# Hybrid attention and mLSTM layer: FFN chunks of three and six token blocks, with Strassen's scheme in gate and up of the six

## The chip, the cores and the metric

One Trainium2 chip, one of its cores. The metric is the device time of one launch in microseconds; the median of three runs of the kernel before is 1618.27 us. Engines: TensorE (PE; PEld is its weight load), VectorE (DVE), ScalarE (ACT), GpSimd (POOL), and SyncE (SP), which issues most DMAs.

## The reference

One transformer layer is applied to 128 context tokens and to 1024 latent tokens, 1152 in all, of width 1024, in float32. Each group of tokens has its own modulation vectors (shift, scale, gate from SiLU of a condition). Cut to what matters:

```python
h = rmsnorm(x, norm1_w) * (1 + sc1) + sh1
aq, ak, av, mq, mk, mv, mo, mg = split(h @ w_in)         # attention and mLSTM inputs
attn_o = attention(rope(norm(aq)), keys, vals)           # 8 query heads of 64, 2 key heads
hm = rmsnorm(mlstm_both_directions(mq, mk, mv, mg)) * sigmoid(mo)
x = x + g1 * (concat([attn_o, hm]) @ w_out)
h2 = rmsnorm(x, norm2_w) * (1 + sc2) + sh2
g, u = split(h2 @ w_gu)                                  # each 1024 -> 2816
x = x + g2 * ((silu(g) * u) @ w_down)                    # 2816 -> 1024
y = rmsnorm(x, final_norm_w)
```

Latent tokens read 128 cached context keys and all 1024 latent keys; context tokens read context keys alone. The keys, values and mLSTM states of the context are outputs too.

## The kernel before

The 1152 tokens are nine blocks of 128 (block 0 is the context). A product of float32 matrices is done in three matmuls of pairs: each factor is split into a high part (`whi`, `aTh`; rounded to fp32r) and a low part (the rest), and high x high, high x low and low x high are added in PSUM. Helper `sub` (L135) computes the low part on VectorE or GpSimd, `load_piece` loads a weight piece into `raw`, copies the high part on ScalarE (L152) and calls `sub`.

Stages, in order: modulation (w_ada) and the first norm; the projection w_in head by head (`head_project`), beside which run the gates of the mLSTM, the rest of w_ada (`ada_rest`) and the mLSTM of the head before (`head_mlstm`); the queries; the mLSTM half of the output projection (`prefill`) beside the attention of the first three blocks. Then the FFN, in three chunks of three token blocks (`CB = 3`, 384 columns). A chunk goes over 22 blocks of 128 hidden features in the groups of `GROUPS`: `gate_up` makes gate and up of one feature block (two weight pieces, 8 k x 3 matmuls of 384 columns each), takes SiLU times up and splits the result into `hl`; `down` multiplies the group's features with w_down, 128 x 512 at a time, and adds the gated result to the residual `x1` (`add_gated`: L997 multiplies from PSUM, L998 adds).

The order of work is written out with generators. `weave(main, side, n_main, n_side)` runs the side's steps spread over the main's. Beside the first four groups of a chunk (17 feature blocks) runs the attention of the next chunk's three blocks; then `attn_out` (attention's half of the output projection), and the next chunk's second norm (`norm2`) beside the last group's `down`. `attention` computes for each head the scores `S` (L918, one buffer of three PSUM banks), the maximum (L920), exp (L921), the rounding to a float16 pair (L924, L925) and two DMA transposes (L928); the values (L942, L943) of a pair of heads come one pair later. The last chunk ends in `down_last`, which takes the last group's down products block by block and finishes each block's norm and store at once. `hot(n)` raises the priority of instructions; a scheduler in the build places each engine's instructions by a simulated timeline, and the order is then fixed.

Buffers are tags in pools: `b0` to `b5` in `hp` hold, one after the other, the first norm's output, the key stacks, the FFN's input pair (`b2`, `b3`) and the residuals (`b4`, `b5`). `raw` has two buffers, `whi` and `wlo` five each. PSUM is four banks `mm`, one `po` and three `S`.

```python
    for c in range(NCH):
        if c + 1 < NCH:
            main = groups(c, cur, GROUPS[:NG])
            ...
            weave(main, chain(previous(c, cur), att), 18 * sum(nf for _, nf in GROUPS[:NG]) - 24, 50)
            emit(att)
            emit(attn_out(c + 1, nxt, oT, out_gates()))
```

Of the kernel before, what the change touches and what calls it, by code (L numbers as in the profile page):

```python
# [8 lines left out]
F32 = mybir.dt.float32  # L9
# [28 lines left out]
LAST = [(0, 5), (5, 5), (10, 4), (14, 4), (18, 4)]  # L38
# [7 lines left out]
def hybrid_step(ctx: ExitStack, tc: tile.TileContext, I: dict, O: dict):  # L46
# [61 lines left out]
    x1_d = [drp.tile([P, D], F32, name=f"x1_d{i}") for i in range(CB)]  # L108

# [9 lines left out]
    def rsqrt(tp, ss, n, inv, cap=24, plus=EPS):  # L119
# [12 lines left out]
        return y  # L132
# [34 lines left out]
    vsc = cp.tile([P, 4], F32, name="vsc")  # L167

# [376 lines left out]
    def norm_rope(qp, cc, ss, x, nb, nh, w, rb):  # L545
# [6 lines left out]
        ssum = qp.tile([P, 20], F32, name=nm("nrs"), tag="nrs", bufs=2)[:, :n]  # L552
# [22 lines left out]
    def k_work(qp, cc, ss, kw):  # L575
# [7 lines left out]
        qone = qp.tile([1, P], F32, name="qone")  # L583
        dve.memset(qone, 1.0)
# [38 lines left out]
    mlp = es1.enter_context(tc.tile_pool(name="mlp", bufs=1, reuse_waits="tile"))  # L623
    mwh = mlp.tile([P, 512], F32, name="mwh")
# [165 lines left out]

    es_r = ExitStack()
# [6 lines left out]
    weave(head_project(1, sts[1]), beside((scan, 1.15), (ada, 0.45)), 56, 56)  # L798
    emit(scan)
    scan = head_mlstm(1, sts[1])  # L800
    weave(head_project(2, sts[2]), beside((scan, 1.15), (ada, 0.55)), 56, 56)
    emit(scan)
    emit(ada)
    es_r.close()
# [23 lines left out]
    kwork = k_work(qp, cc, ss, kw)  # L828
# [3 lines left out]
    emit(kwork)  # L832
    scan = head_mlstm(3, sts[3])
# [32 lines left out]
    ap = ctx.enter_context(tc.tile_pool(name="ap", bufs=1, reuse_waits="tile"))  # L866
    ap2 = ctx.enter_context(tc.tile_pool(name="ap2", bufs=1, reuse_waits="tile"))
    for name, bufs in (("mm", 4), ("po", 1), ("S", 1)):
        psum[name] = ctx.enter_context(tc.tile_pool(name="p" + name, bufs=bufs, space=PSUM, reuse_waits="tile"))
# [7 lines left out]
    def attention(c, oT, done, ha=200, hv=200):  # L877

        late = []
        for i in range(CB):  # L880
            b = c * CB + i
# [17 lines left out]
            for h in range(NQ):  # L899
# [33 lines left out]
                if h % 2 == 1:  # L933
                    def values(phT=phT, plT=plT, kv=kv, nk=nk, b=b, i=i, j=h // 2):
# [26 lines left out]
    att = attention(0, oT, done, 200, 100)  # L961
# [12 lines left out]
    def new_x1(c):  # L974
        x1 = hp.tile([P, CB, D], F32, name=nm("x1"), tag=f"b{4 + c % 2}")
        for i in range(CB):
            if c == 2:
                dma(x1[:, i, :], x1_d[i])
        return [x1[:, i, :] for i in range(CB)]
# [116 lines left out]
    def attn_out(c, a, oT, gs, gx=None, ready=None, then=None, ahead=None):  # L1096

        ws = None
        x1 = a["x1"]
        a["rs"] = []  # L1100
        for i in range(CB):
            while ready is not None and i not in ready:
                yield False
            b = c * CB + i
            if gx is None and i != 1:
                t = ap.tile([P, NQ, P], F32R, name=nm("mx"), tag="qT", bufs=1)
                th, tl = t[:, 0:4], t[:, 4:8]
            else:
                th, tl = mix_spare
            with hot(500):  # L1110
                o = oT[i]
                nc.scalar.copy(th, o)
                sub(tl, o, th.bitcast(F32), "dve" if gx is None else "pool")
            if then is not None and i > 0:
                yield from then(i - 1)
            yield True
            ws = ws or out_pieces(0, spare if gx is not None else None)
            for n in range(2):
                ps = out_block(ws, n, th, tl)
                with hot(200):  # L1120
                    add_gated(x1[i], ps, gx[n] if b == 0 else gs[n], n, pool if gx is not None else dve)
                yield True
            if then is not None:
                with hot(200):
                    a["rs"] += stats(x1[i : i + 1])
        if then is not None:
            yield from ahead
            yield from then(CB - 1)
        else:
            with hot(200):  # L1130
                a["rs"] = stats(x1)
# [9 lines left out]
    def norm2(c, a, i):  # L1141
# [8 lines left out]
        for half in range(2):  # L1150
            with hot(800):
# [6 lines left out]
                for j in range(4):  # L1158
                    k = half * 4 + j
                    if j == 0 and c == 0:  # L1160
# [8 lines left out]
                sub(tl[:, half * 4 : half * 4 + 4, i * P : (i + 1) * P], full, oh.bitcast(F32), "pool" if c == 0 else "dve")  # L1169
            yield True  # L1170

# [52 lines left out]

    def down(c, a, f0, nf, n):
# [26 lines left out]
    def down_last(c, a, f0, nf):  # L1252

        gs, ws = [], []
        fw = ap2.tile([P, D], F32, name="fw", tag="pr", bufs=2)
        dma(fw, I["final_norm_w"].rearrange("(o n) -> o n", o=1).to_broadcast([P, D]))
        for n in range(2):
            pieces = []
            for j in range(0, nf, 2):
                rows = w_down[(f0 + j) * P : (f0 + j + 2) * P, n * 512 : (n + 1) * 512].rearrange("(a p) n -> p a n", p=P)  # L1260
                pieces.append(load_piece([(full_view, rows)], (2, 512)))
            ws.append(pieces)
# [3 lines left out]
        for i in range(CB):  # L1266
            sl = slice(i * P, (i + 1) * P)
            st = ap.tile([P, 4], F32, name=nm("st"), tag="st", bufs=4)
            for n in range(2):
                ps = bank()  # L1270
                for k in range(nf):
                    wh, wl = ws[n][k // 2]
                    ah, al = a["act"][k][0][:, sl], a["act"][k][1][:, sl]
# [14 lines left out]
            nc.scalar.dma_start(yrow(c * CB + i)[:, 0:512], lo)  # L1288
            dma(yrow(c * CB + i)[:, 512:1024], hi)
# [7 lines left out]
    for n in range(2):  # L1297
# [6 lines left out]
                 attn_out(0, cur, oT0, gs, gx, done, lambda i: norm2(0, cur, i),  # L1304
# [8 lines left out]
    oT = []  # L1313
    att = attention(1, oT, set())
# [17 lines left out]
    def previous(c, a):  # L1332

        if c > 0:
            emit(finish(c - 1, a["prev"]))
            yield
        if c == 1:
            a["next"]["x1"] = new_x1(2)
            yield

    cur["next"] = nxt
    for c in range(NCH):
        if c + 1 < NCH:
            main = groups(c, cur, GROUPS[:NG])
            for _ in range(4):
                next(main)
            weave(main, chain(previous(c, cur), att), 18 * sum(nf for _, nf in GROUPS[:NG]) - 24, 50)
            emit(att)
            emit(attn_out(c + 1, nxt, oT, out_gates()))
            emit(groups(c, cur, GROUPS[NG:-1]))  # L1350
            f0, nf = GROUPS[-1]
            emit(gate_up(cur, f0, nf))
            n2 = chain(*[norm2(c + 1, nxt, i) for i in range(CB)])
            weave(chain(down(c, cur, f0, nf, 0), down(c, cur, f0, nf, 1)), n2, 6 * nf, 8)
            emit(n2)
            if c + 2 < NCH:
                oT = []
                att = attention(c + 2, oT, set())
            nxt["prev"] = cur
            cur = nxt  # L1360
            nxt = cur["next"] = {}
        else:
            main = groups(c, cur, LAST[:-1])
            for _ in range(4):
                next(main)
            weave(main, previous(c, cur), 24, 3)
            emit(main)
            emit(gate_up(cur, *LAST[-1]))
            down_last(c, cur, *LAST[-1])
# [52 lines left out]
```

## Time and profile before

| | |
|---|---|
| median of three runs | 1618.27 us (1617.77 to 1619.63) |
| the profiled execution | 1619.03 us, span 1617.1 us |
| mean granted TensorE clock | 0.977 |
| TensorE busy | 1532.5 us, 8670 matmuls |
| VectorE, ScalarE, GpSimd busy | 965.3, 689.8, 618.0 us |
| moved by DMA | 232.71 MB |
| FFN chunks, first product to last | 622 to 975, 977 to 1326, 1326 to 1604 us |

The span goes from the first to the last instruction. Busy time of TensorE counts a matmul from its start to a modelled end, and these overlap, so the pace of matmuls is read from the distance of their starts. A row of a timeline gives start and duration in us, engine, line and operation, output and inputs, shape, and in brackets how long the engine had been idle and for whom it waited.

### The profile page before, as it was taken

Reading aid. Unit: us, or ns where it says so; the run is one execution under the profiler, and the core shown is the slowest. Engines: PE = TensorE matmul, PEld = TensorE weight load, DVE = VectorE, ACT = ScalarE, POOL = GpSimd, SP = SyncE. Lnnn points to the kernel's source line nnn. Section 1 sums busy time; section 2 is a strip of 40 time slices with the busy share of each in tenths; the row PEclk is TensorE's granted clock in tenths of the full one; section 3 lists DMA queues with packets and bytes.
Section 4 is the critical chain, followed back from the end, with each engine's and each line's share of the span. In section 5 each row is a group of like instructions: output and inputs, shape, how many; then the busy total and the mean of one; then the engine's idle time right before and its main releaser. Section 6 shows DMA issues by size and latency. Waiting matters only on the chain. (4 is left out here: it accounts for less than half of the span.)

```text
span 1617.1 us, 23358 instructions
## 1 busy us (share of the span) xinstructions
PE 1532.5 (95%) x8670; PEld 1366.1 (84%) x8670; DVE 965.3 (60%) x1969; ACT 689.8 (43%) x1193; POOL 618.0 (38%) x392
## 2 busy tenths in 40 slices
PE   6899999899898968999999999999999999999996
PEld 2888888898676757998989899898898989999995
DVE  4842363957877668577663646767674474432445
ACT  3522242424534556555643344565552453333322
POOL 1511030413345324443445344444344445544443
PEclk8999999999898988999999999999999999999998
DMA  9244443303155865777773446777684445534441
GB/s 358 67 155 125 117 142 52 82 22 71 50 183 134 180 153 116 174 181 178 180 179 113 148 153 216 188 179 175 156 185 131 131 144 176 151 127 146 144 130 65
DMA packets 386311, 232.71 MB, mean 144 GB/s; under 512 B 169910, under 2 KB 346502, under 8 KB 386198
## 3 DMA queue, kind: packets, MB, share of 16 engines
q1 hardware_dynamic: 384342, 228.04, 52.5%
q10 hardware_dynamic: 1856, 3.19, 0.6%
q8 instruction: 68, 1.11, 0.3%
q14 instruction: 45, 0.37, 0.1%
HBM read 181.16 MB, written 11.69 MB: 119 GB/s over the span
## 5 line engine op out<-in xcount | busy, mean ns | idle before, releaser
L135 POOL TENSOR_TENSOR wlo<-raw,whi 128x1024 fp32r<-128x1024 f32 (+1 forms) x159 | 390.2, 2459 | 512.3 <-ACT whi L152 474.4
L152 ACT CAST whi<-raw 128x1024 fp32r<-128x1024 f32 x239 | 245.0, 1026 | 361.7 <-DMA raw<-in_w_gu_dram 112.8
L1190 PE MATMUL mm<-aTl,whi 128*128 128x384 f32 (+2 forms) x1088 | 363.6, 334 | 0.0
L1189 PE MATMUL mm<-aTh,whi 128*128 128x384 f32 (+2 forms) x1088 | 362.5, 335 | 0.8 <-DVE tn L1217 0.8
L1191 PE MATMUL mm<-aTh,wlo 128*128 128x384 f32 (+2 forms) x1088 | 363.2, 334 | 0.0
L1189 PEld LDWEIGHTS mm<-aTh,whi 128*128 128x128 f32 x1088 | 204.5, 188 | 2.2 <-DVE tn L1217 1.4
L1190 PEld LDWEIGHTS mm<-aTl,whi 128*128 128x128 f32 x1088 | 204.9, 188 | 0.7
L1191 PEld LDWEIGHTS mm<-aTh,wlo 128*128 128x128 f32 x1088 | 204.9, 188 | 0.2
L135 DVE TENSOR_TENSOR wlo<-raw,whi 128x1024 fp32r<-128x1024 f32 (+1 forms) x80 | 98.4, 1230 | 151.7 <-ACT whi L152 147.8
L1008 PE MATMUL mm<-whi,hl 128*128 128x512 f32 x372 | 146.4, 398 | 0.8 <-ACT hl L1221 0.7
L1009 PE MATMUL mm<-wlo,hl 128*128 128x512 f32 x372 | 146.9, 396 | 0.0
L1010 PE MATMUL mm<-whi,hl 128*128 128x512 f32 x372 | 144.3, 396 | 0.8 <-POOL hl L135 0.8
L399 PE MATMUL wi<-whi,hTh 128*128 128x384 f32 (+2 forms) x392 | 135.9, 347 | 5.2 <-ACT hTh L341 5.1
L925 DVE SCALAR_TENSOR_TENSOR pl<-pr,st,ph 128x1152 f16<-128x1152 f32 (+1 forms) x72 | 111.6, 1550 | 47.7 <-ACT ph L924 47.6
L401 PE MATMUL wi<-whi,hTl 128*128 128x384 f32 (+2 forms) x392 | 133.6, 343 | 1.3 <-POOL hTl L135 1.3
L400 PE MATMUL wi<-wlo,hTh 128*128 128x384 f32 (+2 forms) x392 | 133.5, 341 | 0.0
L921 ACT ACTIVATE pr<-S,st 128x1152 f32<-128x1152 f32 (+1 forms) x72 | 81.2, 1128 | 99.7 <-DVE st L920 90.6
L135 POOL TENSOR_TENSOR hl<-tn,hl 128x384 fp32r<-128x384 f32 x66 | 83.5, 1266 | 105.0 <-ACT hl L1221 104.9
L998 DVE TENSOR_TENSOR x<-x,t 128x512 f32<-128x512 f32 x102 | 116.9, 1168 | 0.8
L1217 DVE SCALAR_TENSOR_TENSOR tn<-tn,mm 128x384 f32<-128x384 f32 (+2 forms) x68 | 36.6, 539 | 134.2 <-PE mm L1191 100.4
L918 PE MATMUL S<-kst,qT 128*128 128x384 f32 (+1 forms) x400 | 88.1, 356 | 13.9 <-ACT pr L921 13.8
L920 DVE TENSOR_REDUCE st<-S 128x1 f32<-128x1152 f32 (+1 forms) x72 | 88.8, 1233 | 20.7 <-PE S L918 20.3
(323 smaller groups left out, 2714.2 us busy)
## 6 DMA issues: line engine op xcount, KB each, us to landing
raw<-in_w_gu_dram SPq DMA_DIRECT2D x132, 512.0 KB, 4.0
raw<-in_w_down_dram SPq DMA_DIRECT2D x60, 512.0 KB, 3.6
a<-in_w_ada_dram SPq DMA_DIRECT2D x32, 512.0 KB, 4.2
gl<-g_d SPq DMA_DIRECT2D x36, 256.0 KB, 3.8
aw<-in_w_ada_dram SPq DMA_DIRECT2D x16, 512.0 KB, 8.9
raw<-in_w_in_dram SPq DMA_DIRECT2D x32, 256.0 KB, 5.6
raw<-in_w_out_dram SPq DMA_DIRECT2D x15, 512.0 KB, 4.9
x<-in_x_sample_dram SPq DMA_DIRECT2D x13, 512.0 KB, 6.4
```

Of the source, the lines that this page charges most:

```text
L135: (dve if eng == "dve" else pool).tensor_tensor(out=out, in0=full, in1=hi, op=ALU.subtract)
L152: nc.scalar.copy(hi[:, :n], raw[:, :n])
L399: mm(ps[:, :n], ah, wh[:, k % 2, c0 : c0 + n], start=(k == 0), stop=False)
L400: mm(ps[:, :n], ah, wl[:, k % 2, c0 : c0 + n], start=False, stop=False)
L401: mm(ps[:, :n], al, wh[:, k % 2, c0 : c0 + n], start=False, stop=(k == KD - 1))
L998: eng.tensor_tensor(out=x1[:, cs], in0=x1[:, cs], in1=t, op=ALU.add)
L1008: mm(ps, ah, wh[:, k % 2, :], start=(k == 0), stop=False)
L1009: mm(ps, ah, wl[:, k % 2, :], start=False, stop=False)
L1010: mm(ps, al, wh[:, k % 2, :], start=False, stop=(k == nk - 1))
L1189: mm(ps, wh[:, k, :], th[:, k, :], start=(k == 0), stop=False)
L1190: mm(ps, wh[:, k, :], tl[:, k, :], start=False, stop=False)
L1191: mm(ps, wl[:, k, :], th[:, k, :], start=False, stop=(k == KD - 1))
```

## The change

The first chunk stays as it is (three blocks). The other six blocks become one chunk.

- Attention of all six blocks is woven into the first chunk; its output goes through DRAM (`o_d`). `attn_out_last` then does the output projection of six blocks, and `norm2_pair` the norms, block i with block i + 3.
- Gate and up of the six are a product of 2 x 2 blocks: the weights' columns are (gate, up), their rows the two halves of the 1024 inputs, and the tokens are two halves of 384. It is done by seven half products (4 k each, three float16 matmuls per k) in place of eight. `norm2_pair` makes the seven combinations of the activations once (`hc`), as float16 pairs; `combined` makes for every feature block the seven combinations of the weights; `gate_up_last` adds products in three PSUM banks and the rest by VectorE and ScalarE.
- The pairs are scaled by powers of two, from a bound of the activations and from the largest element of w_gu. `gate_up_max` reads all of w_gu (44 loads of 512 KB) beside the first heads' projections, `gate_up_scales` makes the factors (`gsc`).
- `down_six` uses each piece of w_down for six blocks; `down_last` has six blocks and the last two feature blocks. PSUM becomes eight banks `mm` after the attention.

```diff
-LAST = [(0, 5), (5, 5), (10, 4), (14, 4), (18, 4)]
+LAST = [(0, 4), (4, 4), (8, 4), (12, 4), (16, 4), (20, 2)]
+    def gate_up_max():
+        for t in range(44):
+            raw = wp.tile([P, 1024], F32, name=nm("raw"), tag="raw", bufs=2)
...
+                dma(raw, w_gu[k * P : (k + 1) * P, c * 1024 : (c + 1) * 1024])
...
+            dve.tensor_reduce(out=gmx[:, t : t + 1], in_=raw, axis=AX.X, op=ALU.max, apply_absolute_value=True)
+            yield
...
-    weave(head_project(0, sts[0]), beside((gates, 0.6), (ada, 0.45)), 56, 56)
+    weave(head_project(0, sts[0]), beside((gates, 0.6), (ada, 0.45), (gmax, 0.27)), 56, 56)
...
-    weave(head_project(3, sts[3]), beside((scan, 1.15), (kwork, 0.5)), 56, 56)
+    weave(head_project(3, sts[3]), beside((scan, 1.15), (chain(kwork, gscale), 0.5)), 56, 56)
...
+                            if b >= CB:
+                                dma(o_d[b - CB].rearrange("p (j x) -> p j x", j=4), oT[i])
...
+    def norm2_pair(tp, i, x1, rs, hc, sc, sh):
...
+            split("b11", b11, "pool")
+            sub(t1, b12, b11, "dve")
+            sub(t2_, b22, t1, "dve")
+            split("t2", t2_, "dve")
+            split("t1", t1, "pool")
...
+    def combined(f):
+        raws = []
+        for off in (0, D_FF):
+            raw = (wx if f % 2 else wp).tile([P, 1024], F32, name=nm("raw"), tag="raw", bufs=2)
...
+        w6 = hp.tile([P, 2, 6 * 512], F16, name=nm("w6"), tag=f"b{2 + f % 2}")
+        w1 = wx.tile([P, 2, 512], F16, name=nm("w1"), tag="w1", bufs=2)
...
+        for t in raws:
+            act(t, t, AF.Copy, scale=gsc[:, 1:2])
+        def split(w, cs, src, eng):
+            nc.scalar.copy(w[:, 0, cs], src)
+            sub(w[:, 1, cs], src, w[:, 0, cs], eng)
+        split(w6, slice(0, 1024), g, "pool")
+        dve.tensor_tensor(out=sa[:, lo], in0=u[:, lo], in1=u[:, hi], op=ALU.add)
+        sub(sa[:, hi], sa[:, lo], g[:, lo], "dve")
+        split(w6, slice(1024, 2048), sa, "dve")
+        sub(sb[:, lo], g[:, lo], u[:, lo], "pool")
+        sub(sb[:, hi], g[:, hi], sa[:, hi], "dve")
+        split(w6, slice(2048, 3072), sb, "dve")
+        split(w1, slice(0, 512), u[:, hi], "pool")
...
+    def seven(ps, w, h, first, last):
+        (wh, wl), t = w, h
+        for k in range(4):
+            mm(ps, wh[:, k, :], t[:, 0, k, :], ...)
+            mm(ps, wh[:, k, :], t[:, 1, k, :], ...)
+            mm(ps, wl[:, k, :], t[:, 0, k, :], ...)
+    def gate_up_last(a, hc, f0, nf):
...
+            if f + 1 < NF:
+                a["w"].append(combined(f + 1))
+            x, y, z = (bank()[:, 0:HT] for _ in range(3))
...
+            seven(x, w["a11"], hc["b11"], True, False)
+            nc.scalar.copy(c1, x)
+            seven(y, w["s2"], hc["t2"], True, False)
+            dve.tensor_tensor(out=u2, in0=y, in1=c1, op=ALU.add)
+            seven(z, w["s1"], hc["t1"], True, False)
+            nc.scalar.copy(p5, z)
+            seven(x, w["a12"], hc["b21"], False, True)
+            seven(y, w["s3"], hc["t3"], False, False)
+            dve.tensor_tensor(out=u3, in0=y, in1=c1, op=ALU.add)
+            seven(z, w["s4"], hc["b22"], False, True)
+            seven(y, w["a22"], hc["t4"], False, True)
+            dve.tensor_tensor(out=u2, in0=z, in1=u2, op=ALU.add)
+            dve.tensor_tensor(out=p5, in0=u3, in1=p5, op=ALU.add)
+            dve.tensor_tensor(out=c1, in0=y, in1=c1, op=ALU.add)
...
-            weave(main, chain(previous(c, cur), att), 18 * sum(nf for _, nf in GROUPS[:NG]) - 24, 50)
+    att = attention(range(CB, NB), [], set())
+    weave(main, att, 18 * sum(nf for _, nf in GROUPS[:NG]) - 24, 78)
+    emit(att)
...
+    n2 = chain(*[norm2_pair(np2, i, x1, rs, hc, sc[:, 0], sc[:, 1]) for i in range(CB)])
+    weave(gate_up(cur, f0, nf), n2, 6 * 2 * nf, 6)
+    weave(chain(down(0, cur, f0, nf, 0), down(0, cur, f0, nf, 1)), n2, 6 * nf, 6)
```

After the last sums `gate_up_last` takes, for each half of the tokens, tanh of the gate, one fused add and multiply, a scaled copy, a second fused multiply, the high part and the low part (on GpSimd).

More of the change, by code (lines that the diff above doesn't have):

```diff
@@ L108, in hybrid_step @@
     x1_d = [drp.tile([P, D], F32, name=f"x1_d{i}") for i in range(CB)]
+    o_d = [drp.tile([P, 512], F32, name=f"o_d{i}") for i in range(LB)]
     ident = cp.tile([P, P], F32, name="ident")
@@ L875, in hybrid_step, with attention @@
         sub(vs[:, i0 : i0 + 5, :, 1], v, vs[:, i0 : i0 + 5, :, 0], "pool")
-    def attention(c, oT, done, ha=200, hv=200):
+    def attention(blocks, oT, done, ha=200, hv=200):
         late = []
-        for i in range(CB):
-            b = c * CB + i
+        for i, b in enumerate(blocks):
             nk = 1 if b == 0 else NB
@@ L1094, in prefill, with attn_out @@
                     yield
-    def attn_out(c, a, oT, gs, gx=None, ready=None, then=None, ahead=None):
+    def attn_out(a, oT, gs, gx, ready, then, ahead):
         ws = None
@@ L1101, in attn_out @@
         for i in range(CB):
-            while ready is not None and i not in ready:
+            while i not in ready:
                 yield False
[L1104 to L1109, printed above, removed]
+            th, tl = mix_spare
             with hot(500):
@@ new lines, in hybrid_step @@
+    main = groups(0, cur, GROUPS[:NG])
+    for _ in range(4):
+        next(main)
+    weave(main, att, 18 * sum(nf for _, nf in GROUPS[:NG]) - 24, 78)
+    emit(att)
+    es_at.close()
+    psum["mm"] = ctx.enter_context(tc.tile_pool(name="p8", bufs=8, space=PSUM, reuse_waits="tile"))
+    np1 = ctx.enter_context(tc.tile_pool(name="np1", bufs=1, reuse_waits="tile"))
+    es_n = ExitStack()
+    np2 = es_n.enter_context(tc.tile_pool(name="np2", bufs=1, reuse_waits="tile"))
+    late_x1 = np1.tile([P, CB, D], F32, name="late_x1")
@@ new lines, in hybrid_step @@
+    for i in range(CB):
+        dma(late_x1[:, i, :], x1_d[i])
+    x1 = nxt["x1"] + [late_x1[:, i, :] for i in range(CB)]
+    pairs = [hp.tile([P, 2, 2, 4, HT], F16, name=nm("hc"), tag=f"b{i}") for i in range(2)]
+    hc = {"b11": pairs[0][:, 0], "t2": pairs[0][:, 1], "t1": pairs[1][:, 0], "b21": pairs[1][:, 1]}
+    for n in ("t3", "b22", "t4"):
+        hc[n] = np1.tile([P, 2, 4, HT], F16, name="hc_" + n)
+    sc = np1.tile([P, 2, KD], F32, name="sc")
+    dve.tensor_scalar(out=sc[:, 0], in0=scale2[:, :, 1], scalar1=gsc[:, 0:1], scalar2=None, op0=ALU.mult)
@@ new lines, in hybrid_step, with groups_last @@
+    emit(n2)
+    es_n.close()
+    wx = ctx.enter_context(tc.tile_pool(name="wx", bufs=1, reuse_waits="tile"))
+    last = {"x1": x1}
+    last["w"] = [combined(0)]
+    def groups_last():
+        for f0, nf in LAST[:-1]:
+            yield from gate_up_last(last, hc, f0, nf)
+            yield from down_six(last, f0, nf, 0)
+            yield from down_six(last, f0, nf, 1)
+    main = groups_last()
+    for _ in range(4):
+        next(main)
+    weave(main, finish(0, cur), 24, 3)
+    emit(main)
@@ L1372 @@
+    emit(gate_up_last(last, hc, *LAST[-1]))
+    down_last(last, *LAST[-1])
 TC_OPTS = dict(schedule_with_timeline_sim=True)
```

292 lines of the change are left out of this document (211 added, 81 removed).

## The prediction

> **What bounds the kernel now.** I read the page's busy times and slices first, then the table of stages, then the timeline of TensorE for the pace of single matmuls, then the engines beside it.
>
> ```profile
> span 1617.1 us, 23358 instructions
> ...
> PE 1532.5 (95%) x8670; PEld 1366.1 (84%) x8670; DVE 965.3 (60%) x1969; ACT 689.8 (43%) x1193; POOL 618.0 (38%) x392
> ...
> PE   6899999899898968999999999999999999999996
> ...
> PEclk8999999999898988999999999999999999999998
> ```
>
> The execution took 1619.0 us, 1.9 more than its span; the median of the runs is 1618.3, so a change of the span is taken over one to one. From slice 17 on (about 640 us) TensorE is busy all the time at full granted clock. The table of stages says the same (columns: busy us and instructions of each engine, clock, DMA share, GB/s):
>
> ```profile
> 80.00:120.00 40.00, 40.00 (x248) 32.65 (x247) 18.42 (x55) 9.75 (x24) 5.12 (x9) 1.00 0.53 165
> ...
> 280.00:320.00 40.00, 35.18 (x220) 31.87 (x218) 36.37 (x126) 17.80 (x61) 17.47 (x25) 1.00 0.26 71
> ...
> 560.00:600.00 40.00, 30.14 (x159) 24.59 (x158) 24.82 (x47) 23.00 (x30) 13.38 (x8) 0.83 0.76 177
> ...
> 1000.00:1040.00 40.00, 37.12 (x195) 32.32 (x194) 24.81 (x33) 20.68 (x26) 20.66 (x9) 1.00 0.78 223
> ...
> 1040.00:1200.00 160.00, 159.34 (x928) 147.00 (x927) 114.57 (x157) 92.80 (x121) 63.64 (x29) 1.00 0.74 174
> 1400.00:1560.00 160.00, 160.00 (x845) 149.71 (x844) 65.03 (x76) 52.53 (x66) 75.50 (x39) 1.00 0.44 135
> ```
>
> 1040 to 1200 is the second FFN chunk with the third chunk's attention woven in, 1400 to 1560 the third chunk alone. Both lose under 1 us of TensorE. Fewer or shorter matmuls there come off the end directly, as long as the other engines keep up. A busy TensorE can hide small gaps, so the pace is read from starts (start, us, engine, line):
>
> ```profile
> 1203.89 0.34 PE L1189 MATMUL mm<-aTh,whi 128*128 128x384 f32 x1
> ...
> 1213.60 0.34 PE L1191 MATMUL mm<-aTh,wlo 128*128 128x384 f32 x1
> ...
> 561.76 0.27 PE L942 MATMUL po<-phT,vs 128*128 128x256 f16 x1
> ...
> 563.40 0.27 PE L943 MATMUL po<-plT,vs 128*128 128x256 f16 x1
> ...
> 1601.34 0.39 PE L1274 MATMUL mm<-whi,hl 128*128 128x512 f32 x1
> ...
> 1603.90 0.40 PE L1276 MATMUL mm<-whi,hl 128*128 128x512 f32 x1
> ```
>
> 57 gate/up matmuls of 384 columns start in 9.71 us: 0.1734 us each. 16 float16 matmuls of 256 columns start in 1.64 us: 0.1093 each. 12 down matmuls of 512 columns: 0.2327 each.
>
> **The products.** Removed: two chunks x 22 feature blocks x 48 matmuls = 2112 at 0.1734, 366.2 us. Added: 22 x 7 half products x 4 k x 3 = 1848 float16 matmuls of 384 columns. No row has float16 at 384; the nearest, scaled by columns, gives 0.164 each, 303.1 us. Gain 63 us. If float16 were no faster than the present pairs at this size, 320.4 us and a gain of 46; if part of the 0.1093 is fixed per instruction, a little over 63. I take 63. The Trainium skill (TensorE: Matmul & The Clock Gate, Back-to-back issue gap) gives columns over 2.4 GHz plus 2.5 ns, 109.2 ns at 256, which the trace bears out; by it the 1848 would take 300 us and the gain be 66.
>
> Down products, output projection and attention keep their matmuls; only their order changes. With one FFN chunk fewer there is one change of chunk fewer: TensorE stood 2.9 us in 1000 to 1040. I count -3.
>
> **The vector work of the six-block chunk.** Strassen's sums replace matmuls by additions. Durations of their kinds, alone and beside GpSimd:
>
> ```profile
> 1400.13 1.05 ACT L152 CAST whi<-raw 128x1024 fp32r<-128x1024 f32 x1 [2.76 <-DMA raw<-in_w_gu_dram]
> ...
> 1404.50 0.51 ACT L1221 CAST hl<-tn 128x384 fp32r<-128x384 f32 x1
> ...
> 1404.67 2.40 POOL L135 TENSOR_TENSOR wlo<-raw,whi 128x1024 fp32r<-128x1024 f32 x1 [5.21 <-ACT whi L152]
> ...
> 1407.03 1.02 POOL L135 TENSOR_TENSOR hl<-tn,hl 128x384 fp32r<-128x384 f32 x1
> ...
> 1401.21 1.23 DVE L135 TENSOR_TENSOR wlo<-raw,whi 128x1024 fp32r<-128x1024 f32 x1 [4.32 <-ACT whi L152]
> ...
> 1402.36 0.55 DVE L1217 SCALAR_TENSOR_TENSOR tn<-tn,mm 128x384 f32<-128x384 f32 x1
> ...
> 1596.22 0.69 DVE L998 TENSOR_TENSOR x<-x,t 128x512 f32<-128x512 f32 x1
> ...
> 1597.78 1.81 DVE L998 TENSOR_TENSOR x<-x,t 128x512 f32<-128x512 f32 x1
> ...
> 1597.76 1.29 POOL L1283 TENSOR_TENSOR x<-x,fw 128x512 f32<-128x512 f32 x1 [7.30 <-ACT jk L1280]
> ```
>
> Per feature block TensorE needs 84 x 0.164 = 13.8 us of products. In `combined` and after the products GpSimd has one subtraction of 1024, two of 512 and two of 384: 2.40 + 2.58 + 2.04 = 7.0 us. VectorE has three sums of 512 (2.1), two splits of 1024 (2.5) and five two-input steps of 384 on SBUF (2.8), 7.3 us, and four sums that read PSUM (2.2). ScalarE: five passes of 1024 (5.3), about 0.6 for one of 512, eight of 384 (4.1): 10.0. Each engine alone fits in 13.8. But the pair of rows at 1597.8 shows an addition of two SBUF operands, 0.69 alone, take 1.81 when a GpSimd subtraction of 1.29 runs: it waited for it. If the two engines exclude each other so, 7.0 + 7.3 = 14.3 us stand against 13.8, and 16.5 if nothing of the PSUM sums fits beside GpSimd. Over a group of four blocks the down products (4 x 36 x 0.2327 = 33.5 us) add twelve additions (8.3) and four splits (some 8): 57.2 + 16.3 = 73.5 of 88.7 us of TensorE, so the mean fits, and one block's weights can be made ready during the down products, but the buffers b2/b3 hold two blocks' weights and no more. There is also a tight place: `u3` must leave bank y within the seven's 12 matmuls (2.0 us) before the next product adds to it, and VectorE, strictly in order, may stand behind a split or a wait for GpSimd; TensorE then waits, and all behind it. Bounds: 0 (in 1400 to 1560 VectorE and GpSimd together are busy 140.5 of 160 us and TensorE lost nothing) to 16.5 - 13.8 = 2.7 x 22 = 59 us. I take 0.8 us a block, 17 us, nearer to the first end because that row has the same kind of load.
>
> **Attention in one stretch.** Six blocks are now woven into chunk 0's first 17 feature blocks, 78 steps over the same main work where 50 were.
>
> ```profile
> L920 DVE TENSOR_REDUCE st<-S 128x1 f32<-128x1152 f32 (+1 forms) x72 | 88.8, 1233 | 20.7 <-PE S L918 20.3
> ...
> phT<-ph SPq DMA_TRANSPOSE x19, 3.4
> plT<-pl SPq DMA_TRANSPOSE x19, 4.5
> ...
> raw<-in_w_gu_dram SPq DMA_DIRECT2D x26, 512.0 KB
> raw<-in_w_down_dram SPq DMA_DIRECT2D x12, 512.0 KB, 3.6
> ```
>
> The transposes are those of 1040 to 1200, the loads those of 1400 to 1560. 19 heads in 160 us are 8.4 us a head. After: 17 x (48 x 0.1734 + 18 x 0.2327) = 212.7 us of FFN and 6 x (48 x 0.1734 + 72 x 0.1093) = 97 of attention, 310 us for 48 heads, 6.5 a head. A head costs VectorE (114.57 - 0.41 x 121.6) / 19 = 3.4 us, where 121.6 us is the FFN's share of those 160 (less 19 x 97 / 48) and 0.41 is VectorE's share in 1400 to 1560; the same way the DMA engines 3.4 (0.74 against 0.44). With the FFN beside it (4.4 us at 0.41 and 0.44) VectorE is at 5.2 of 6.5, DMA at 5.4. Both fit, but the slack between a pair's scores and its values shrinks by 4 us against a chain of reduce, exp, two roundings and a transposition of 4.5. Bounds: 0, as now, to 25 us (in 560 to 600, attention with little beside it, TensorE lost a quarter). I take 7.
>
> **The maximum of w_gu.** 44 loads of 512 KB and 44 reductions in 80 to 330 us. A load takes 0.44 x 160 / 39 = 1.8 us of the DMA engines (79 in all; the row of 80 to 120 has a share of 0.53, that of 280 to 320 one of 0.26); a reduction about 1.1 by the 1152 wide one (48 in all). VectorE has room in the first of these rows (18 of 40), hardly any in the second (36 of 40). SP issues these loads in order: one that waits for its `raw` buffer, that is for VectorE, holds the head weights and w_ada behind it. The scales' two reductions and dozen of short steps go into the same price. 0 to 20; I take 5.
>
> **The change of chunk.** `attn_out_last` has the matmuls of two `attn_out`; its loads of `o_d` and `late_x1` go beside 33 us of them. `norm2_pair` is woven into 62 us of chunk 0's last group. The first product needs all three pairs and the first combined weights, whose `w1` lies where norm2's tiles were. 0 to 8; I take 2.
>
> **The tail.** Six blocks with two feature blocks each, where there were three with four:
>
> ```profile
> 1587.41 0.39 PE L1274 MATMUL mm<-whi,hl 128*128 128x512 f32 x1
> ...
> 1599.52 0.68 DVE L997 TENSOR_TENSOR t<-mm,gl 128x512 f32<-128x512 f32 x1
> ...
> 1603.86 0.68 DVE L997 TENSOR_TENSOR t<-mm,gl 128x512 f32<-128x512 f32 x1
> ...
> 1612.63 0.75 DVE L1287 SCALAR_TENSOR_TENSOR x<-x,ry,fw 128x512 f32<-128x512 f32 x1
> ```
>
> Now the end comes 29.7 us after the first of these matmuls. TensorE's 16.8 us stay. VectorE takes 4.3 us a block (between the second and third row), more than the 2.8 us in which TensorE will deliver one: 2.8 + 5 x 4.3 + 9.5 (the last block's own chain, 1603.86 to 1613.38) + 3.7 to the end = 37.5, so +8; and with two feature blocks the last one's activations are wanted after a half, not three quarters, of the products. +6 to +16; I take +10.
>
> **Sum.** -63 - 3 + 17 + 7 + 5 + 2 + 10 = -25: 1594 for the profiled execution, 1593 for the median.
>
> **The rivals.** (a) All vector work hidden, no stall in the chunk and none in the attention: -63 - 3 + 2 + 2 + 8 = -54, 1564. For it: 140.5 of 160 busy and no loss today. Against it: only two weight buffers. (b) The pair VectorE and GpSimd sets the pace of the chunk of six: 16.5 us a block, +59 in place of 17, so +17: 1635, slower. It decides from 1.9 us a block on. For it: 1.81 for 0.69 beside GpSimd, and 14.3 against 13.8 even when packed. Against it: the down products' slack. The Trainium skill (SBUF — State Buffer, SBUF: two separate sides) calls this an exclusive lock held for a whole instruction, and those two rows agree. (c) Attention at 6.5 us a head no longer fits: TensorE loses 25 + 17 of the gain and the early stage its 20: 1626. (d) Float16 at 384 columns is no faster than now: 46 in place of 63, 1610.
>
> **How the numbers follow.** Forecast 0.45, (a) 0.23, (b) 0.20, (c) 0.06, (d) 0.06. About 0.2% (3 us) is what a measurement of this kernel can tell from no change. Forecast and (a), with most of (d), are faster: 0.71; 0.04 falls within 0.2%; slower 0.25. The range runs from (a) to just short of (b)'s full price: 1562 to 1632. The forecast's own range is 1575 to 1612.
>
> **What would show it.** Starts of the new products 0.162 to 0.165 apart, about 13.8 us a feature block. Waits of TensorE in the chunk of six, by VectorE's sums (y, u3) or by weights not yet split: 17 us in all; over 42 and (b) holds. Between chunk 0's start and its end, waits for `pr`, `phT` or `plT`: 7. From the first matmul of `down_last` to the end: 40 us. The forecast is wrong if the products start further apart than 0.17, if the six-block chunk's blocks take over 15.7 us, or if the stage before 450 us grows by more than 20.

## The result, and the profile after

The changed kernel takes 1719.19 us (median of four runs, 1712.37 to 1725.65) where the kernel before takes 1618.95 on the same chip: 1.0615 times as long, 95% interval 1.0564 to 1.0666. The forecast was 1593. It is slower by 100 us; even the top of the range, 1632, is far off.

The page of the changed kernel (its profiled execution took 1712.37 us):

```profile
span 1710.6 us, 23079 instructions
...
PE 1501.9 (88%) x8410; PEld 1196.6 (70%) x8410; DVE 1198.0 (70%) x2241; ACT 756.0 (44%) x1337; POOL 577.7 (34%) x394
...
PE   6898697889986887999999856996999999999993
...
PEclk8999899899998999999999967998999999999997
```

TensorE is busy 31 us less and VectorE 233 us more. The row of slices (42.8 us each, counted from 0) no longer has its unbroken stretch: there are new dips in slices 4 and 6 (171 to 299 us), in 23 and 24 (984 to 1069) and in 27 (1155 to 1197). The stages, in columns as before; the first row is the kernel before, all others the changed one:

```profile
160.00:200.00 40.00, 40.00 (x274) 35.18 (x269) 14.84 (x54) 7.51 (x26) 1.22 (x5) 1.00 0.40 109
```

```profile
160.00:200.00 40.00, 27.78 (x162) 23.70 (x160) 16.34 (x32) 1.14 (x3) 0.00 (x0) 0.90 0.84 182
```

```profile
735.00:960.00 225.00, 222.73 (x1280) 202.64 (x1279) 162.35 (x222) 130.18 (x170) 83.71 (x40) 1.00 0.84 184
960.00:1045.00 85.00, 46.87 (x229) 35.58 (x227) 47.99 (x74) 37.97 (x48) 7.94 (x4) 0.74 0.70 154
...
1153.00:1200.00 47.00, 34.07 (x175) 18.51 (x174) 44.76 (x58) 29.08 (x42) 20.96 (x13) 0.82 0.50 146
1200.00:1661.00 461.00, 443.77 (x2382) 296.11 (x2381) 345.42 (x403) 202.03 (x292) 194.19 (x110) 1.00 0.24 71
1661.00:1710.00 49.00, 20.37 (x90) 14.61 (x87) 36.03 (x115) 15.53 (x35) 9.61 (x8) 0.76 0.17 65
```

The reader is to see four places where TensorE stands: the early stage, 960 to 1045 (the end of the attention; the last product beside it is at 972), 1153 to 1200 (the change of chunk, with VectorE busy 44.76 of 47 us) and the tail. The long stretches, 735 to 960 and the six-block chunk from 1200, are nearly full.

I put a number on each place by the starts of TensorE's matmuls: length of the stage less the matmuls in it at their full pace (0.1627 us a float16 matmul of 384 columns, 0.1734 an fp32r one; a few records are missing, so these are rough).

| place | forecast | measured |
|---|---|---|
| 1848 float16 products for 2112 | -63 | -65 |
| one change of chunk fewer | -3 | -3 (taken as forecast, not measured apart) |
| maximum of w_gu: first gate/up product at 622.6 us before, 664.1 after | +5 | +41 |
| attention in one stretch (68 us lost in 664 to 1045, about 18 in the two such stretches before) | +7 | +50 |
| change of chunk (26 us lost in 1080 to 1200) | +2 | +24 |
| six-block chunk, 1200 to 1661 | +17 | +17 waits, +24 by the pace |
| tail, first down product of `down_last` to the end: 29.7 before, 49.1 after | +10 | +19 |

The right-hand column, with 24 for the chunk, adds to +90; the span of the two profiled executions grew by 93.5. The line at 1200 is drawn by hand: 18.6 of the 26 us of the change of chunk are lost from 1153.5 on, when the first feature blocks of the six-block chunk already run. Counted from there, the chunk lost 42 us.

The new products themselves do what was said of them:

```profile
1360.01 0.33 PE L1377 MATMUL mm<-hc,w 128*128 128x384 f16 x1
...
1365.37 0.33 PE L1377 MATMUL mm<-hc_t,w 128*128 128x384 f16 x1
```

The second start is the 33rd after the first: 5.36 us, 0.1624 each. (The Trainium skill, TensorE: Matmul & The Clock Gate, Back-to-back issue gap, gives 162.5 ns for 384 columns; the trace agrees.)

### The profile page after: what moved, and what is told of

Same layout as the page of the kernel before. It is cut to its first block, busy times and chain, and to the rows that moved or that the text cites. A ratio compares the mean times of both kernels' runs of the same rounds, so it can differ in the third digit from the quotient of the medians.

```text
span 1710.6 us, 23079 instructions
## 1 busy us (share of the span) xinstructions
PE 1501.9 (88%) x8410; PEld 1196.6 (70%) x8410; DVE 1198.0 (70%) x2241; ACT 756.0 (44%) x1337; POOL 577.7 (34%) x394
## 5 line engine op out<-in xcount | busy, mean ns | idle before, releaser
L138 POOL TENSOR_TENSOR wlo<-raw,whi 128x1024 fp32r<-128x1024 f32 x80 | 198.1, 2479 | 485.3 <-ACT whi L155 480.6
L155 ACT CAST whi<-raw 128x1024 fp32r<-128x1024 f32 (+1 forms) x121 | 124.3, 1031 | 119.8 <-DMA raw<-in_w_in_dram 38.6
L973 DVE SCALAR_TENSOR_TENSOR pl<-pr,st,ph 128x1152 f16<-128x1152 f32 (+1 forms) x72 | 112.4, 1561 | 52.2 <-ACT ph L972 51.8
L138 POOL TENSOR_TENSOR w<-raw,w 128x1024 f16<-128x1024 f32 (+1 forms) x44 | 91.7, 2086 | 159.1 <-ACT w L1357 155.9
L1303 PE MATMUL mm<-aTl,whi 128*128 128x384 f32 (+2 forms) x384 | 127.5, 332 | 0.0
L1304 PE MATMUL mm<-aTh,wlo 128*128 128x384 f32 (+2 forms) x384 | 127.2, 332 | 0.0
L1302 PE MATMUL mm<-aTh,whi 128*128 128x384 f32 (+2 forms) x384 | 126.9, 332 | 0.0
L1377 PE MATMUL mm<-hc,w 128*128 128x384 f16 x352 | 115.3, 330 | 5.7 <-ACT hc L1263 4.1
L1378 PE MATMUL mm<-hc,w 128*128 128x384 f16 x352 | 116.1, 330 | 0.0
L1379 PE MATMUL mm<-hc,w 128*128 128x384 f16 x352 | 115.3, 330 | 0.0
L1454 PE MATMUL mm<-whi,hl 128*128 128x512 f32 x240 | 93.2, 403 | 12.1 <-ACT hl L1426 7.4
L968 DVE TENSOR_REDUCE st<-S 128x1 f32<-128x1152 f32 (+1 forms) x72 | 88.8, 1233 | 18.7 <-PE S L966 18.0
L1044 DVE TENSOR_TENSOR t<-mm,gl 128x512 f32<-128x512 f32 x118 | 78.3, 683 | 30.7 <-PE mm L1089 11.2
L990 PE MATMUL po<-phT,vs 128*128 128x256 f16 x292 | 77.4, 296 | 22.5 <-DMA phT<-ph 11.6
```

Of the source, the lines that this page charges most:

```text
L138: (dve if eng == "dve" else pool).tensor_tensor(out=out, in0=full, in1=hi, op=ALU.subtract)
L155: nc.scalar.copy(hi[:, :n], raw[:, :n])
L1302: mm(ps, wh[:, k, :], th[:, k, :], start=(k == 0), stop=False)
L1303: mm(ps, wh[:, k, :], tl[:, k, :], start=False, stop=False)
L1304: mm(ps, wl[:, k, :], th[:, k, :], start=False, stop=(k == KD - 1))
L1377: mm(ps, wh[:, k, :], t[:, 0, k, :], start=(first and k == 0), stop=False, skip_group_check=True)
```

## The experiments

All are the changed kernel with the edit shown. Each time is a median of four runs, each ratio one to the kernel before, which ran beside it (1619 to 1621 us); 1.0615 is the changed kernel. Two ratios differ if their intervals do not meet.

### The maximum of w_gu

**No maximum.** The 44 loads and reductions replaced by `dve.memset(gmx[:, 0:44], 0.17)`; the scale then doesn't come from the data.

> The changed kernel without the 44 loads and reductions for the largest weight; the maximum is set to the constant 0.17, so the scale is not taken from the weights. Theory (the maximum costs the stage of the head projections 42 us, the distance by which the first gate/up product came later): about 1677 us, first gate/up product near 622 us, not 664. Rival (that stage was late for another reason, such as the smaller buffers of the square roots): it stays near 1719.

1689.24 us, 1.0427 (1.0412 to 1.0443): 30 us back, 12 fewer than the first expectation. The first gate/up product comes at 634.2, where 622 was expected.

**Reductions without loads, loads without reductions.**

```diff
-            dma(raw, w_gu[...]); dve.tensor_reduce(out=gmx[:, t : t + 1], in_=raw, ...)
+            dve.tensor_reduce(out=gmx[:, t : t + 1], in_=<1024 numbers of hTh[0]>, ...)   # first kernel
+            dma(raw, w_gu[...])                                                           # second kernel
```

> The 44 reductions stay on VectorE at their places, but they read a part of the first norm's output that lies in SBUF; nothing is loaded, so the scale is taken from other numbers. Theory (VectorE, in order, stood with a reduction at its head that waited for its load: 70 us of idle time before the reductions): most of the 42 us come back, about 1680 to 1690, and the reductions wait for nothing. Rival (the 54 us of VectorE work itself delays the mLSTM's steps): 1705 or more.

> The 44 loads stay, the reductions go, the maximum is the constant 0.17. Theory (VectorE's wait): 1677 to 1690. Rival (the 22 MB on the DMA engines, or SP standing at a load that waits for its buffer with the head weights behind it): 1705 or more. If both this and the run without loads come near 1680, neither the work nor the loads cost it alone, and it is the wait of the one for the other.

Reductions alone: 1708.98 us, 1.0536 (1.0517 to 1.0556). Loads alone: 1721.12, 1.0626 (1.0602 to 1.0649), as slow as with both. So the loads are enough to cost it all. The first of the two is less clear than it looks: with nothing to wait for, the reductions were placed in one lump, and TensorE lost time at another place than in the changed kernel (below). The first gate/up product comes at 642.0, 8 us later than in the run without a maximum. That run is 20 us faster in all; where the other 12 us go is open.

```profile
80.00:120.00 40.00, 29.79 (x181) 26.57 (x180) 40.00 (x46) 5.50 (x12) 4.98 (x9) 0.87 0.47 142
```

**Small loads.** As loads alone, but each brings 64 of its 1024 columns: `dma(raw[:, 0:64], w_gu[k * P : (k + 1) * P, c * 1024 : c * 1024 + 64])`.

> The 44 loads for the maximum stay in their places, in the same queue and the same two raw buffers, but each brings 32 KB instead of 512 KB, and the reductions are left out (the maximum is a constant, as in the run with loads alone, 1721). If the moved bytes cost the time (the DMA engines busy 0.84 to 0.92 at 160 to 200 us), the queries end near 470 us and the kernel takes 1685 to 1695, like the run without any of it (1689). If the order in SyncE's queue or the shared raw buffers cost it, nothing comes back: queries end near 495 to 510, 1712 to 1725.

1705.54 us, 1.0523 (1.0489 to 1.0557). Neither expectation holds: half of it comes back. What the main DMA queue moved from 80 to 330 us (packets, MB, share of 16 engines) in the kernel before, the changed kernel, and this one:

```profile
q1 hardware_dynamic: 40987, 27.85, 40.7%
```

```profile
q1 hardware_dynamic: 40445, 47.36, 70.3%
```

```profile
q1 hardware_dynamic: 43828, 27.50, 41.6%
```

The bytes are back to those of before, and the first gate/up product comes at 650.4, between 634.2 (none) and 660.4 (whole loads): some 10 to 16 us are the bytes (by this start, and by the times) and 16 are the places that the loads hold.

**Another queue.** `dma` for these loads became `nc.scalar.dma_start`, so that no head weight stands behind them on SyncE.

> As the changed kernel, but the 44 loads for the maximum are issued by ScalarE, so that no head weight stands behind them in SyncE's queue; bytes, raw buffers and reductions stay. If the order in SyncE's queue is the cost, the queries end 20 us or more earlier than 509 us and the kernel takes 1690 to 1700. If it is the bytes or the two raw buffers, 1710 to 1728, and ScalarE's own waits may add some.

1722.99 us, 1.0648 (1.0622 to 1.0673): nothing back. This does not clear the order in SyncE's queue, since the waits moved along with the loads. From 80 to 330 us, in the changed kernel, SyncE stands at these loads (L800), and everything issued after them with it:

```profile
SPq L800 <- DMA raw<-in_w_gu_dram: 50.5, 22, 7.5
...
SPq L800 <- DVE gmx L804: 15.7, 15, 1.6
```

With the loads on ScalarE's queue, ScalarE's own steps wait behind them, and the head weights (L154, still on SyncE) wait for a `raw` buffer that the loads hold:

```profile
ACT kt L654 <- DVE gmx L804: 25.1, 2, 16.2
...
ACT part L377 <- DMA raw<-in_w_gu_dram: 21.4, 1, 21.4
```

```profile
SPq L154 <- DMA raw<-in_w_gu_dram: 18.3, 3, 13.0
SPq L154 <- DVE gmx L804: 16.2, 3, 14.3
```

So both kinds of place are seen to hold something up, a queue's order and the two shared buffers; how the 16 us divide between them stays open. Loads with buffers of their own were not tried.

**The maximum from chunk 0's own pieces.** No extra loads: `load_piece` in chunk 0 takes one more `dve.tensor_reduce` of each raw piece of w_gu, and the weights' factor is made after the last.

> The 44 extra loads are gone: the maximum is taken from the raw weight pieces of w_gu that chunk 0 loads anyway (44 reductions on VectorE in 665 to 1120 us), and the weights' factor is made after the last of them. If the extra loads were the cost of the early stage, it comes back as in the run without any maximum (first gate/up product near 634 us) and the kernel takes 1692 to 1703. If VectorE's reductions beside the attention lengthen each head's chain (above 7.6 us a head), half of that is lost again: 1704 to 1716.

1736.9 us, 1.0716 (1.0687 to 1.0745): worse than both expected. The early stage came back in part (first gate/up product at 645.6, where 634 was expected), but chunk 0 paid more than that: this is an experiment on the attention, below.

### The attention

**More cover.** The last group's gate and up of chunk 0 is put beside the attention as well: `chain(groups(0, cur, GROUPS[:NG]), gate_up(cur, *GROUPS[-1]))`, and norm2 beside that group's `down` alone.

> The gate and up products of chunk 0's last group (five feature blocks, 41 us of TensorE) are put beside the attention too; the second norms of the six blocks then go beside that group's down products alone. Theory (attention cannot go faster than 7.5 us a head beside the FFN, so 62 us of it were left over with TensorE half idle from 960 to 1045): some 35 to 40 us of these are covered; the norms lose 5 to 15 of cover: 1690 to 1705. Rival (the rest of the attention is slow of itself, by the transposes): no gain, 1715 or more.

1706.56 us, 1.0529 (1.0513 to 1.0544): 13 back, between the two expectations. Two heads are left over when the gate/up products end (1028), where there were 13 (943); but norm2 then lacks its cover, and the first Strassen product comes only 8 us earlier (1145.5).

**Attention written denser.** 112 steps in place of 78 over the same products: `weave(main, att, ... - 24, 112)`.

> The six blocks' attention is woven into chunk 0 at 112 steps where 78 were, nothing else. If the heads left over at 972 us are there because the products were written ahead of them, heads come some 6 us apart, none is left over, and 25 to 35 us come back: 1685 to 1695. If a head's own chain of waits (scores, reduce, exp, rounding, transposition, one S buffer) sets 7.5 us a head beside the products, nothing moves: 1710 to 1722.

1735.89 us, 1.0726 (1.0708 to 1.0744): slower by 17, outside both expectations. One maximum (L968) is taken for each head; the groups' rows count them in 735 to 940 us, in the changed kernel and in this one:

```profile
L968 DVE TENSOR_REDUCE st<-S 128x1 f32<-128x1152 f32 x27 | 36.4, 1349 | 1.3 <-PE S L966 1.2
```

```profile
L968 DVE TENSOR_REDUCE st<-S 128x1 f32<-128x1152 f32 x25 | 33.8, 1351 | 8.8 <-PE S L966 8.7
```

27 heads in 205 us are 7.6 us a head. Written denser they are no closer, 8.2. By the starts of its matmuls, TensorE loses 27 us from the first gate/up product to the last product beside the attention, 17 in the changed kernel; its longest waits there are at the value products, 7.7 us in all. The heads cannot be hurried from there.

**No low part of the probabilities.** Leaves out per head the VectorE pass L973, one transposition and 9 matmuls.

> Leaves out the low parts of the probabilities: per head one VectorE pass (1.4 to 2.1 us), one DMA transposition (1.3 to 1.9) and 9 matmuls of 0.109 us. The chain scores, maximum, exp, next scores stays. If that chain sets the 7.5 us a head beside the products, heads stay at 7.0 or more and the time falls little: 1698 to 1716. If VectorE's or the DMA engines' load sets it, heads come at 6.3 us or less, none is left over, and the kernel takes 1645 to 1670.

1699.19 us, 1.0492 (1.0476 to 1.0508), at the edge of the chain's 1698 to 1716. The same row, 735 to 940 us:

```profile
L966 DVE TENSOR_REDUCE st<-S 128x1 f32<-128x1152 f32 x27 | 36.6, 1354 | 30.9 <-PE S L964 30.7
```

VectorE now waits 30.7 us for scores, and yet there are 27 heads again. Neither VectorE's nor the DMA engines' load sets the pace. The products end at 946 instead of 972, since 292 matmuls are gone, and 11 heads are left over then, 10 in the changed kernel; the time that came back needs no faster head. In the run with chunk 0's maximum the count is 24 (8.5 us a head):

```profile
L960 DVE TENSOR_REDUCE st<-S 128x1 f32<-128x1152 f32 x24 | 32.4, 1349 | 4.1 <-PE S L958 4.0
```

Its 21 other reductions there stand between links of the chain in VectorE's fixed order, 1.2 us each and 15.9 us of waiting for the weights that they read:

```profile
L157 DVE TENSOR_REDUCE bcol<-raw 128x1 f32<-128x1024 f32 x21 | 25.5, 1215 | 15.9 <-DMA raw<-in_w_gu_dram 15.9
```

One head of the changed kernel (timeline):

```profile
900.50 1.29 PE L966 MATMUL S<-kst,qT 128*128 128x384 f32 x6
...
902.82 1.35 DVE L968 TENSOR_REDUCE st<-S 128x1 f32<-128x1152 f32 x1
...
904.20 1.23 ACT L969 ACTIVATE pr<-S,st 128x1152 f32<-128x1152 f32 x1 [0.90 <-DVE st L968]
...
908.28 1.22 PE L966 MATMUL S<-kst,qT 128*128 128x384 f32 x6
```

Scores, maximum and exp take 1.3, 1.4 and 1.2 us; 1.0 goes by behind a pass on VectorE, and 2.8 until TensorE, in its written order, comes to the next scores. `S` has one buffer, so no head starts before the exp of the one before. Of the 7.6 us some 2 come with the products: the ten heads that are left over at 972 follow each other 5.5 us apart, though TensorE then runs at a lower clock (0.74).

### The change of chunk and the tail

**Group of two first, `finish` later.** `LAST = [(0, 2), (2, 4), (6, 4), (10, 4), (14, 4), (18, 4)]`, and `finish` starts 12 steps later.

> In the six-block chunk the group of two feature blocks comes first instead of last, and the end of chunk 0 (finish) is written 12 steps later. If the tail's extra is the last activations coming late and the 7 us wait at 1175 is finish's vector steps, the last down products to the end take 40 to 43 us where 49 were and the first Strassen products 10 us less: 1695 to 1706. If the tail is paced by VectorE's 4.3 to 4.9 us for each of six blocks and the wait is only passed on, 1710 to 1720.

1709.07 us, 1.0561 (1.0529 to 1.0593); the interval meets that of the changed kernel, so the gain of 10 is not sure, and the time lies between the two expectations. The tail takes 51.3 us, but now holds 33.5 us of down matmuls where it held 16.8. Waits of TensorE from 1125 to 1300 us, total, times and longest:

```profile
PE mm L1377 <- DVE u L1404: 4.8, 1, 4.8
PE mm L1377 <- ACT hc L1263: 4.0, 1, 4.0
PE mm L1379 <- DVE w L138: 3.3, 1, 3.3
PE mm L1454 <- ACT c L1418: 3.3, 1, 3.3
```

In the changed kernel the first of these was 7.3 and the second 4.1. With `finish` out of the way other steps of VectorE fill its place.

**No GpSimd in the chunk's gate and up.** Leaves out GpSimd's low parts of a11, a12, a22 and of the activations in `hl`, and its sum of 512; the high part is multiplied twice, so all matmuls stay. The expectation below names b11, t1, b21 and b22 too, but the edit does not touch `norm2_pair`: the trace still has its 12 steps on GpSimd, and the low parts of w_down are left there as well.

> Leaves GpSimd's subtractions out of the six-block chunk's gate and up and of its norm (the low parts of a11, a12, a22, b11, t1, b21, b22 and of the activations, and one sum of 512): the high part is used twice there, so the number of matmuls stays. VectorE keeps its own steps, less none. If VectorE and GpSimd holding each other up is what the stalls of the chunk (16.9 us of TensorE waits after 1200) and the 24 us at the change of chunk come from, 20 to 35 us come back: 1685 to 1699. If the waits are the order of the steps on VectorE and ScalarE's last step before the down products, at most 12: 1707 to 1722.

1683.65 us, 1.0408 (1.0377 to 1.044): 35 us back, as much as the first expectation had at most; between the profiled executions it is 30. The first Strassen product comes at the same time (1153.4), which says nothing of the norm, whose GpSimd steps stayed; the last comes 26 us earlier. The wait of 7.3 us for `u` is gone, and the waits from 1200 on fall from 16.9 to 6.7. VectorE's groups, 1153 to 1661 us, in the changed kernel:

```profile
L1417 DVE SCALAR_TENSOR_TENSOR tn<-tn,p 128x384 f32<-128x384 f32 x21 | 29.3, 1393 | 7.9 <-ACT tn L1416 7.9
...
L138 DVE TENSOR_TENSOR sa<-sa,raw 128x512 f32<-128x512 f32 x22 | 28.0, 1277 | 0.4
...
L1404 DVE TENSOR_TENSOR u<-mm,c 128x384 f32<-128x384 f32 x22 | 12.2, 553 | 39.0 <-PE mm L1379 39.0
...
L1484 DVE SCALAR_TENSOR_TENSOR x<-x,ry,fw 128x512 f32<-128x512 f32 x6 | 8.9, 1550 | 0.0
```

and with those steps left out (two of the rows are one line further down):

```profile
L138 DVE TENSOR_TENSOR sa<-sa,raw 128x512 f32<-128x512 f32 x22 | 17.2, 784 | 0.4
...
L1418 DVE SCALAR_TENSOR_TENSOR tn<-tn,p 128x384 f32<-128x384 f32 x22 | 15.8, 720 | 7.2 <-ACT tn L1417 7.1
...
L1405 DVE TENSOR_TENSOR u<-mm,c 128x384 f32<-128x384 f32 x22 | 12.2, 555 | 50.5 <-PE mm L1380 50.5
...
L1484 DVE SCALAR_TENSOR_TENSOR x<-x,ry,fw 128x512 f32<-128x512 f32 x6 | 4.1, 748 | 0.0
```

The same steps with two operands in SBUF take 1393, 1277 and 1550 ns beside GpSimd's steps and 720, 784 and 748 without them; the step that reads one operand from PSUM takes 553 and 555.

### All together

Chunk 0's maximum, more cover, the group of two first, `finish` later; then the same with a constant for the maximum.

> Chunk 0's maximum, chunk 0's last gate and up beside the attention too, the group of two first and finish later, all together. If the three losses are separate, their gains add: 1719 - 20 to 30 - 13 - 10 = 1666 to 1676. If they hide each other (a stage only waits for the next late thing), 1680 to 1695. In neither case below before's 1619.

> As the run before it, but with a constant in place of the maximum: no loads and no reductions for it at all. It shows what the maximum still costs there. Gains that add: 1719 - 30 - 13 - 10 = 1666, within 1660 to 1672; the 44 reductions in chunk 0 then cost 0 to 10.

1714.62 us, 1.0587 (1.0556 to 1.0617), missing both expectations, and 1665.17, 1.0281 (1.0264 to 1.0299), as the sum of the single gains said (1666). As far as this sum shows, the losses are separate and add. The 49 us between the two are the maximum's, for which 0 to 10 was expected: the last head's scores start at 1044 in the one and 1001 in the other, and the first Strassen product comes at 1164.2 and 1113.7. The reductions in chunk 0 are not all of it, since TensorE also stands for the factor that is made after the last of them:

```profile
PE mm L117 <- DVE gt L1593: 12.5, 1, 12.5
```

Not even the one without a maximum comes near the kernel before.

## Why the prediction was wrong, point by point

**The products: right.** 0.164 was taken, 0.1624 measured, and the gain is 65 us. Rival (d) is out.

**The maximum of w_gu: the largest miss in proportion.** The term was "0 to 20; I take 5"; the early stage grew by 41 us, past the 20 named as what would make the forecast wrong. I added up what the DMA engines and VectorE had free over 250 us and found room. The stage has its own order instead: the head weights go through the same queue and the same two `raw` buffers, and they come late, partly by the bytes (10 to 16 us), partly by the places that the loads hold there (16). Of the 41, 30 go with the maximum. The other 11 lie between the queries' end (468.0 us without the maximum, 465.8 before, by the start of its last product) and the first gate/up product (634.2 and 622.6); their cause is open.

**Attention: the step that failed is "Both fit".** The term compared loads, VectorE 5.2 and DMA 5.4 of 6.5 us a head. Heads came 7.6 us apart beside products whatever was taken off either engine; that this is the pace of a chain is by exclusion of the two loads. 24 heads in 205 us were to be counted in the trace of before:

```profile
L920 DVE TENSOR_REDUCE st<-S 128x1 f32<-128x1152 f32 x24 | 32.4, 1351 | 6.0 <-PE S L918 6.0
```

There TensorE was full and the pace did no harm; 8.4 us a head was read as slack. With one chunk's products as cover in place of two, 10 heads are left over at 972 us, when the last product beside them ends (13 at 943, when the gate/up products end), and run with little beside them, and the way of their output through DRAM is a wait of its own. Waits of TensorE from 972 to 1046 us:

```profile
PE S L966 <- ACT pr L969: 12.5, 4, 3.7
...
PE mm L1087 <- ACT mx L1185: 9.9, 1, 9.9
PE po L990 <- DMA phT<-ph: 9.0, 2, 8.6
```

Rival (c) was this mechanism, given 0.06 and priced at 25 + 17 + 20; measured are 50 for the attention and 41 early. Without products beside it the chain took 5.5 us a head; how much of the rest is the order in which TensorE's work was written stays open. Only 13 of the 50 us came back with more cover, so the rest is not shown to be the cover's.

**Change of chunk: "0 to 8; I take 2" was 24.** I named the matmuls beside which the work of the change would go, not the engine that does it: VectorE was busy 44.76 of 47 us. 11 of these 24 us go with GpSimd's steps in gate and up: without them the loss from 1153 to 1200 falls from 18.6 to 7.2.

**Vector stalls: 17 forecast; 16.9 of waits from 1200 on, but 42 us lost in the whole chunk.** That the first two numbers meet is in part where the line was drawn. By the starts of the matmuls, TensorE lost 18.6 us before 1200 and 23 to 24 after, 1.9 us a feature block in place of 0.8: just at the mark that the prediction set for (b). The place was off too: `u3` costs about 1 us, and 7.4 are the first down product of a group waiting for ScalarE's last rounding of `hl`. The step that failed is the choice of the stage from 1400 to 1560 as the nearer bound, and with it the price of 0.56 us for a step of 384 with two SBUF operands, where the row shown for this size reads PSUM: beside GpSimd such a step took 1.39. Rival (b) at its full price of 59 is out, while its mechanism, the two engines holding each other up, is shown by these durations. Taking GpSimd's steps away gave 30 us between the profiled executions, 11 before 1200, 15 after and 3 in the tail; 1.6 us of it at most are TensorE's own waits for GpSimd's results in 1200 to 1661. (The Trainium skill, SBUF — State Buffer, SBUF: two separate sides, lets VectorE be blocked only in a perf mode of two ports or with two SBUF inputs; the row with a PSUM operand, 553 against 555 ns, agrees.)

**Tail: +10 forecast, +16 as the upper bound, +19 measured.** VectorE's first step on their sums comes 12 us after the first of these matmuls, where it came after 8 before; the last step of the activations on VectorE now starts 6.7 us after that matmul, where it started after 0.9. Then VectorE runs at 4.3 to 4.9 us a block, where 4.3 was worked out.

So the gain came as forecast. Three terms that were priced at 5, 7 and 2 us (the maximum, the attention, the change of chunk) cost 41, 50 and 24.

## What to carry to other kernels

An engine at half load says nothing of how fast a chain through it can go: count how many units (heads, pieces) the trace shows in a stretch and take that as the pace, until a run shows it faster. When a change takes away matmuls, ask which chain they covered, and how much cover is left per unit. Loads and sums for a small side result cost what they hold up, shared buffers and places in an engine's order, and a stage with free engine time can still have none to give.

## What the runs showed of the hardware

A wait can be paid twice. After waits of TensorE, matmuls ran at half pace in parts of the leftover attention:

```profile
991.12 0.42 PE L990 MATMUL po<-phT,vs 128*128 128x256 f16 x1
...
993.68 0.42 PE L990 MATMUL po<-phT,vs 128*128 128x256 f16 x1
```

The second start is the 12th after the first, 0.213 us each, where the same ones took 0.109 beside the products. The granted clock from 985 to 994 us is 0.50, after an idle stretch of 3.7 us at 978; that of 960 to 1045 is 0.74. The prediction had no term for it. (The Trainium skill, TensorE: Matmul & The Clock Gate, Part 1, halves the clock after an idle window and gives columns over 1.2 GHz, 213 ns at 256; the trace agrees.)
